# Second stage of dilated attention: bias tables through SP, values written in token order by PE, merge sums on POOL, last merge by PE

## The chip, the cores and the metric

The kernel runs on one core of a Trainium2 chip. The metric is the device time of one execution in microseconds (us). Three runs of the kernel before took 2099.55, 2100.16 and 2105.69 us; their median, 2100.16, is the number to which the changed kernel is compared.

## The reference

Two layers on 1024 tokens of 1024 channels, in float32. Layer 0 is a gated short convolution. Layer 1, to whose second half the change belongs, is a dilated attention in three groups of 16 heads of 64 channels:

```python
proj = h @ w_in                                   # h = rms_norm(x, attn_norm)
for g, (window, dilation) in enumerate(((128, 1), (512, 4), (2048, 16))):
    q = rms_norm(qkv[:, :, g, 0], q_gain[g]); k = rms_norm(qkv[:, :, g, 1], k_gain[g])
    o, l = dilated_group_attention(q, k, qkv[:, :, g, 2], bias_g, window, dilation)
    outs.append(o); lses.append(l)                # l: log of the softmax denominator
alpha = jax.nn.softmax(stack(lses), axis=0)
o = sum(alpha[..., None] * stack(outs), axis=0)
y = o * silu(z)
x = x + y @ w_out
```

In each group a query sees the keys t - dilation * j for j from 0 to 128, so that the tokens of one residue class form a dense sequence with a causal band, worked in blocks of 128 queries with a learned bias per distance. The three groups' outputs are merged with weights that come from their softmax denominators, gated by silu(z), and multiplied by w_out.

## The kernel before, in words

**First stage (to about 1645 us).** The convolution layer and the projections of the attention layer run as large matrix products. Their results are written to DRAM: q and k of each head pair and group to `qkd`, values to `vd`, the gate to `zd`, the residual stream to `x1d`. The change does not touch this stage, and the order of instructions on every engine is the same up to its end.

**Second stage.** It is written out by hand in the order of a software pipeline: inside `tc.manual_schedule` each engine runs its instructions in the order of the code. The work is 8 head pairs (two heads on partitions 0 to 63 and 64 to 127) x 3 groups = 24 units. Groups 0 and 1 have four steps per unit (two query blocks each), group 2 two (four blocks each), so that a pair has 10 steps and the whole 80. The code calls the parts of a step at different lags. In iteration k it issues

- A of step k (L886 to L897): PE multiplies q and k into a PSUM tile `ps`; DVE adds the bias table `bt` and takes the minimum in one instruction per query block (L894); ACT takes the exponential and its row sum (L897);
- C of step k - 3 (L915): PE multiplies the values `V` with the transposed probabilities `pts` into `po`; every half of a unit, `finish` copies `po` to the SBUF tile `o` (L928, L930, L933). Rows of groups 1 and 2 are in the order of the residue classes, and this copy puts them into token order, with strides in its output;
- the merge of earlier pairs at larger lags (below);
- B of step k - 2 (L904): PE transposes the probabilities, and DVE or ACT copies them to `pts` (L843, L845);
- one tile of the output product (`some`, L1035 to L1037), if there is one in this iteration;
- the loads that begin here: q, k, V and the gate (`loads`, L829 to L835) on SP's queue six steps ahead of their unit, the bias tables (`prefetch`, L858) on POOL's queue four steps ahead. Every unit has its own bias tables, two of 128 x 256 (128 x 128 in group 2).

**The merge of a pair.** The row minima and sums (`nl`) of groups 0 and 1 are stored to DRAM (`nld`, L940, L943) and read back in the order of group 2 (`ml`, L938), at `finish` of the unit's second half. `weights` (L952 to L956) and `shares` (L965 to L970) make on DVE three weights per token and head, `fo`. POOL writes them to DRAM (`fd`, L971) and reads them back six times, spread over 64 partitions (`fb`, L976). `merge` multiplies each group's output by its `fb` (group 0 on POOL, L982; groups 1 and 2 on DVE, L984), adds the three on DVE (L987, L988) and multiplies by the gate (L989), in halves of 512 tokens; `split_y` divides the result into a high and a low part for the output product (ACT L993, DVE L994). These calls stand 11 to 14 steps behind the last step of the pair; the last pair has weights and shares earlier and merges both halves in `last`.

**Output product.** The rows of w_out are split into a high part (ACT, L62) and a low part (DVE, L63). The product runs in three passes over 16 tiles of 128 x 512: pairs 0 to 3 (12 matmuls a tile, from step 55), pairs 4 and 5 (6 matmuls, from step 75), and, after the last step, pairs 6 and 7 (6 matmuls). In the first two passes a tile's partial sum is read from `x1d` (L1054, four tiles ahead, on SP), increased on DVE (L1062) and written back (L1070, on POOL's queue). They use one PSUM buffer, `pd`. In the last pass the sum goes to the output (L1134, L1135), and the load of the partial sum four tiles on follows behind the output's DMA in SP's queue.

Of the kernel before, what the change touches and what calls it, by code (L numbers as in the profile page):

```python
# [35 lines left out]
def trunk(ctx: ExitStack, tc: tile.TileContext, a, out):  # L36
# [22 lines left out]
    def split_row(raw):  # L59
        lo = wp.tile([P, 1024], F32R, name="wlo", tag="wlo", bufs=4)  # L60
        hi = wp.tile([P, 1024], F32R, name="whi", tag="whi", bufs=4)
        nc.scalar.activation(hi, raw, AF.Copy)  # L62
        nc.vector.tensor_tensor(lo, raw, hi.bitcast(F32), op=OP.subtract)  # L63
        return hi, lo
# [752 lines left out]
    with tc.tile_pool(name="sp", bufs=3, space=PSUM) as sp, tc.tile_pool(name="ptp", bufs=2, space=PSUM) as ptp, \  # L817
# [29 lines left out]
        def attention(hp, g):  # L847
# [4 lines left out]
            def prefetch():  # L852
# [3 lines left out]
                for s in range(2):  # L856
                    b0 = ap.tile([P, 256], F32, name="bt", tag="bt", bufs=6)
                    nc.gpsimd.dma_start(b0[:, :n], sk[2 * hp + s, 127:127 + P * w]  # L858
                                        .rearrange("(i m) -> i m", m=w)[:, :n])
                    bt.append(b0)  # L860
# [8 lines left out]
            def make(js, first):  # L869
# [3 lines left out]
                def A():  # L873
# [5 lines left out]
                    for n, j in enumerate(js):  # L879
                        alone = g == 2 or (j == 0 if g == 0 else j % 2 == 0)  # L880
                        x0, nk = (n if g == 2 else 2 * n), 1 if alone else 2
                        vb = [j] if alone else [j - 1, j]
                        kv = slice(vb[0] * P, (j + 1) * P)
                        for s, hs in enumerate((lo, up)):
                            out_ = ps[s][:, x0:x0 + nk].rearrange("p a b -> p (a b)")
                            nc.tensor.matmul(out_, q[hs, j * P:(j + 1) * P], k[hs, kv], start=True, stop=True)  # L886
# [21 lines left out]
                def C():  # L908
                    if js[0] % 4 == 0:
                        u["po"] = opp.tile([P, 4, P], F32, name="po", tag="po")  # L910
                    po = u["po"]
                    V = VS[hp, g]
                    for i, (x, j, vb, f, l) in enumerate(c):
                        for s, hs in enumerate((lo, up)):
                            nc.tensor.matmul(po[hs, j % 4], V[:, vb, hs], pts[s][:, i], start=f, stop=l)  # L915
                    if js[-1] % 4 == 3:
                        finish(js[-1] // 4)
# [3 lines left out]
            def finish(q):  # L921

                if q == 0:
                    O[hp, g] = ap.tile([P, S], F32, name="o", tag="o", bufs=6)
                o = O[hp, g]
                for i in range(4):
                    if g == 0 and i == 0:
                        nc.vector.tensor_copy(o[:, q * HALF:q * HALF + HALF], u["po"].rearrange("p a b -> p (a b)"))  # L928
                    elif g == 1 and i % 2 == 0:
                        nc.vector.tensor_copy(o.rearrange("p (n s c) -> p c n s", n=2, c=4)[:, 2 * q + i // 2],  # L930
                                              u["po"][:, i:i + 2])
                    elif g == 2 and i == 0:
                        nc.vector.tensor_copy(o.rearrange("p (i r) -> p r i", r=8)[:, 4 * q:4 * q + 4], u["po"])  # L933
                if q == 0:
                    return
# [5 lines left out]
                elif g == 1:  # L941
                    for n in range(2):
                        nc.gpsimd.dma_start(nld[hp, :, 1].rearrange("(n s c) e -> n s c e", n=2, c=4)[n],  # L943
                                            u["nl"].rearrange("p (c n) e -> p n c e", n=2)[:, n])
# [14 lines left out]
            def shares():  # L959
# [4 lines left out]
                fo = sm.tile([P, 3, 2, 8], F32, name="fo", tag="fo", bufs=1)  # L964
# [5 lines left out]
                nc.vector.tensor_tensor(fo.rearrange("p w s r -> p r w s"), f, mx.to_broadcast([P, 8, 3, 2]), op=OP.mult)  # L970
                nc.gpsimd.dma_start(fd[hp].rearrange("w s (i r) -> i w s r", r=8), fo)  # L971
                for w in range(G):
                    fb = fbp.tile([P, S], F32, name="fb", tag="fb")
                    u["fb", w] = fb
# [3 lines left out]
            def merge(hf, i):  # L978

                o = [O[hp, w][:, half(hf)] for w in range(G)]  # L980
                if i == 0:
                    nc.gpsimd.tensor_tensor(o[0], o[0], u["fb", 0][:, half(hf)], op=OP.mult)  # L982
                    for w in (1, 2):
                        nc.vector.tensor_tensor(o[w], o[w], u["fb", w][:, half(hf)], op=OP.mult)  # L984
                else:
                    z = SZ[hp][:, half(hf)]
                    nc.vector.tensor_tensor(o[1], o[1], o[2], op=OP.add)  # L987
                    nc.vector.tensor_tensor(o[1], o[1], o[0], op=OP.add)  # L988
                    nc.vector.tensor_tensor(z, o[1], z, op=OP.mult)  # L989

            def split_y(hf):
                hi, lo = y2[hp][:, 0, half(hf)], y2[hp][:, 1, half(hf)]
                nc.scalar.activation(hi, SZ[hp][:, half(hf)], AF.Copy)  # L993
                nc.vector.tensor_tensor(lo, SZ[hp][:, half(hf)], hi.bitcast(F32), op=OP.subtract)  # L994

            def last(hf):
                if hf == 0:
                    y2[hp] = ap.tile([P, 2, S], F32R, name="y2", tag="y2", bufs=5)
                merge(hf, 0)
                merge(hf, 1)  # L1000
                split_y(hf)

            def ready():
                y2[hp] = ap.tile([P, 2, S], F32R, name="y2", tag="y2", bufs=5)
                for hf in range(2):
                    split_y(hf)

            steps = []
            for q in range(2):
                for js in ([[4 * q, 4 * q + 1, 4 * q + 2, 4 * q + 3]] if g == 2 else  # L1010
                           [[4 * q, 4 * q + 1], [4 * q + 2, 4 * q + 3]]):
                    st = make(js, not steps)
                    steps.append(dict(zip((0, LB, LC), st)))
                    if g == 2 and q == 1:
                        lw, ld = LC + (1 if hp == HP - 1 else 2), LC + 8
# [188 lines left out]
```

## Time and profile before

| what | value |
|---|---|
| runs of the kernel before | 2099.55, 2100.16, 2105.69 us |
| the profiled execution: own time / span | 2105.98 / 2103.9 us |
| mean granted clock of TensorE | 0.97 |
| busy share of the span: PE, DVE, ACT, POOL | 94%, 71%, 43%, 44% |
| second stage: from the first reduction (L894) to the end | 1652.35 to 2103.9 us |

The profile gives for each group of instructions its busy time, the mean of one, and the idle time ahead of it with what ended that idle time. The windows give the same by stretches of time, with the clock granted to TensorE and the share of time in which the DMA engines were busy. The shares over the whole span say little here: PE's 94% come from the first stage, and the change acts in the last 450 us alone. A busy time of PE is modelled, and a matmul counts as longer when the clock is lower.

### The profile page before, as it was taken

Reading aid. Unit: us, or ns where it says so; the run is one execution under the profiler, and the core shown is the slowest. Engines: PE = TensorE matmul, PEld = TensorE weight load, DVE = VectorE, ACT = ScalarE, POOL = GpSimd, SP = SyncE. Lnnn points to the kernel's source line nnn. Section 1 sums busy time; section 2 is a strip of 40 time slices with the busy share of each in tenths; the row PEclk is TensorE's granted clock in tenths of the full one; section 3 lists DMA queues with packets and bytes.
Section 4 is the critical chain, followed back from the end, with each engine's and each line's share of the span. In section 5 each row is a group of like instructions: output and inputs, shape, how many; then the busy total and the mean of one; then the engine's idle time right before and its main releaser. Section 6 shows DMA issues by size and latency. Waiting matters only on the chain.

```text
span 2103.9 us, 29100 instructions
## 1 busy us (share of the span) xinstructions
PE 1981.9 (94%) x9998; PEld 1599.0 (76%) x9998; DVE 1499.2 (71%) x2796; ACT 906.5 (43%) x2048; POOL 915.7 (44%) x889
## 2 busy tenths in 40 slices
PE   7999899999999999999999999999999877779976
PEld 6887688888888888788888887888888655557754
DVE  6865675666757465888996889788888466667674
ACT  5433333333335353444344343443433666665540
POOL 0456666666663113344554445444445322223331
PEclk9999999999999999999999999999999998889988
DMA  5325412112216464233332233323333565577757
GB/s 183 111 82 152 113 71 75 65 66 76 71 66 210 164 221 135 95 101 120 97 125 80 101 121 104 97 101 100 120 105 118 191 170 165 155 203 228 239 148 239
DMA packets 119619, 272.59 MB, mean 130 GB/s; under 512 B 16958, under 2 KB 17726, under 8 KB 119472
## 3 DMA queue, kind: packets, MB, share of 16 engines
q1 hardware_dynamic: 90720, 180.56, 26.0%
q0 software_dynamic: 28752, 90.18, 14.8%
q8 instruction: 78, 1.28, 0.2%
q14 instruction: 69, 0.57, 0.1%
HBM read 203.01 MB, written 76.05 MB: 133 GB/s over the span
## 4 chain that ended last, share of the span: by engine, by line
PE 60%; DVE 13%; issue 5%; DMA 5%; ACT 4%; POOL 1%; SPq 0%; DVEq 0%; ACTq 0%; POOLq 0%
PE pp L306 15%; PE pp L309 15%; PE pp L308 14%; PE pp L557 3%; PE pp L558 3%; PE pp L556 3%; PE po L915 2%; DVE ws L172 2%; DMA bt<-sk 2%; ACT xs L897 2%; PE pt L904 2%; PE ps L886 1%; DVE blkc L713 1%; DVE xs L894 1%; DVE ri L74 1%
## 5 line engine op out<-in xcount | busy, mean ns | idle before, releaser
L172 DVE TENSOR_TENSOR ws<-wr,ws 128x512 fp32r<-128x512 f32 x284 | 270.1, 953 | 130.8 <-ACT ws L171 129.4
L171 ACT ACTIVATE ws<-wr 128x512 fp32r<-128x512 f32 x284 | 178.6, 630 | 390.1 <-PE pp L309 230.3
L281 POOL TENSOR_TENSOR sr<-wr 128x512 f32<-128x512 f32 x136 | 185.8, 1366 | 253.2 <-DMA wr<-in_conv_w_in 58.2
L171 ACT ACTIVATE ws<-sr 128x512 fp32r<-128x512 f32 x272 | 169.4, 629 | 292.4 <-PE pp L309 243.9
L172 DVE TENSOR_TENSOR ws<-sr,ws 128x512 fp32r<-128x512 f32 x272 | 234.2, 868 | 83.8 <-ACT ws L171 82.2
L897 ACT ACTIVATE xs<-xs,nl 128x128 f32<-128x128 f32 (+1 forms) x384 | 168.1, 439 | 128.6 <-DVE nl L894 128.0
L318 DVE TENSOR_TENSOR f<-pp,f 128x512 f32<-128x512 f32 x204 | 139.6, 684 | 83.8 <-PE pp L309 79.1
L894 DVE CUSTOM_DVE_ANT_0 xs<-ps,bt 128x128 f32<-128x128 f32 (+1 forms) x384 | 111.2, 348 | 79.8 <-DMA bt<-sk 45.9
L314 ACT ACTIVATE f<-pp 128x512 f32<-128x512 f32 x228 | 132.4, 581 | 24.8 <-POOL blkc L685 11.4
L915 PE MATMUL po<-pts,V 128*64 128x128 f32 x1120 | 98.5, 302 | 38.8 <-DVE pts L843 27.5
L915 PEld LDWEIGHTS po<-pts,V 128*64 128x64 f32 x1120 | 72.8, 149 | 72.1 <-DVE pts L843 39.4
L718 POOL DMA_DIRECT2D qkd<-blkc x96 | 68.1, 716 | 135.2 <-DVE blkc L713 127.8
L281 POOL TENSOR_TENSOR sr<-wr,sr 128x512 f32<-128x512 f32 x68 | 89.5, 1316 | 83.3 <-issue 59.3
L886 PE MATMUL ps<-qk 64*128 64x128 f32 (+1 forms) x768 | 97.6, 366 | 28.0 <-DVE nl L894 27.9
L676 ACT ACTIVATE f<-f 128x512 f32<-128x512 f32 x96 | 60.7, 633 | 137.3 <-DVE f L318 100.5
L306 PE MATMUL pp<-blke,ws 128*128 128x512 f32 x272 | 108.4, 399 | 7.2 <-ACT f L314 7.2
L306 PE MATMUL pp<-blkg,ws 128*128 128x512 f32 x272 | 107.6, 396 | 4.3 <-ACT f L314 3.2
L308 PE MATMUL pp<-blkg,ws 128*128 128x512 f32 x272 | 106.8, 393 | 3.3 <-DVE blkg L526 3.3
L306 PE MATMUL pp<-blkf,ws 128*128 128x512 f32 x272 | 108.5, 399 | 0.7 <-ACT f L314 0.7
L308 PE MATMUL pp<-blke,ws 128*128 128x512 f32 x272 | 107.7, 396 | 0.0
L306 PE MATMUL pp<-blka,ws 128*128 128x512 f32 x272 | 107.1, 394 | 0.7 <-ACT f L314 0.7
L306 PE MATMUL pp<-blkb,ws 128*128 128x512 f32 x272 | 107.5, 395 | 0.0
(298 smaller groups left out, 5532.8 us busy)
## 6 DMA issues: line engine op xcount, KB each, us to landing
wr<-in_conv_w_in SPq DMA_DIRECT2D x128, 256.0 KB, 2.8
wr<-in_wqk SPq DMA_DIRECT2D x96, 256.0 KB, 3.0
qkd<-blkc POOLq DMA_DIRECT2D x96, 256.0 KB, 3.2
qk<-qkd SPq DMA_DIRECT2D x48, 512.0 KB, 6.7
wr<-in_conv_w_out SPq DMA_DIRECT2D x64, 256.0 KB, 3.1
f<-in_x SPq DMA_DIRECT2D x48, 256.0 KB, 4.7
wr<-in_wv SPq DMA_DIRECT2D x48, 256.0 KB, 2.9
vd<-f POOLq DMA_DIRECT2D x48, 256.0 KB, 2.4
```

Of the source, the lines that this page charges most:

```text
L171: nc.scalar.activation(t[:, 0], src, AF.Copy)
L172: nc.vector.tensor_tensor(t[:, 1], src, t[:, 0].bitcast(F32), op=OP.subtract)
L281: nc.gpsimd.tensor_tensor(t, x, y, op=op)
L306: nc.tensor.matmul(ps, w[:, 0, ws], b[:, k, 0], start=new and k == 0, stop=False, skip_group_check=not new)
L308: nc.tensor.matmul(ps, w[:, 0, ws], b[:, k, 1], start=False, stop=False, skip_group_check=not new)
L309: nc.tensor.matmul(ps, w[:, 1, ws], b[:, k, 0], start=False, stop=end and k == 3, skip_group_check=not new)
L314: nc.scalar.activation(t, ps, AF.Copy)
L318: nc.vector.tensor_tensor(m, ps, m, op=OP.add)
L886: nc.tensor.matmul(out_, q[hs, j * P:(j + 1) * P], k[hs, kv], start=True, stop=True)
L894: nc.vector.tensor_tensor_reduce(out=x, in0=ps[s][:, x0:x0 + nk].rearrange("p a b -> p (a b)"), in1=u["bt"][s][:, bs], op0=OP.add, op1=OP. ...
L897: nc.scalar.activation(x, x, AF.Exp, bias=nm, scale=-1.0, accum_out=L)
L915: nc.tensor.matmul(po[hs, j % 4], V[:, vb, hs], pts[s][:, i], start=f, stop=l)
```

## The change

Six things change, all in the second stage.

1. The bias tables go through SP's queue, ahead of q, k and V of their own unit, six steps before it begins (before: POOL's queue, four steps).

In SP's queue, at the loads of three units in the middle of the stage, stood before (`qk` are q and k, two DMAs; `sz` is the gate):

```order
L829 DMA qk<-qkd 128x1024 x2
L832 DMA V<-vd 128x512 x2
L835 DMA sz<-zd 128x1024
L829 DMA qk<-qkd 128x1024 x2
L832 DMA V<-vd 128x512 x2
```

and now, for the same units (`sk_83`, `sk_84` and `sk_85` are the bias tables of groups 0, 1 and 2):

```order
L831 DMA qk<-qkd 128x1024 x2
L834 DMA V<-vd 128x512 x2
L837 DMA sz<-zd 128x1024
L860 DMA bt<-sk_83 128x256 x2
L831 DMA qk<-qkd 128x1024 x2
L834 DMA V<-vd 128x512 x2
L860 DMA bt<-sk_84 128x256 x2
```

Each unit's two bias DMAs now stand in SP's queue between the previous unit's loads and its own.

In POOL's queue, from the shares of one pair to those of the next, stood before:

```order
L971 DMA fd<-fo 128x6x8
L976 DMA fb<-fd 64x1024 x6
L940 DMA nld<-nl 128x8x4
L858 DMA bt<-sk_83 128x256 x2
L943 DMA nld<-nl 512x1x4 x2
L982 TENSOR_TENSOR o<-o,fb 128x512
L858 DMA bt<-sk_84 128x256 x2
L982 TENSOR_TENSOR o<-o,fb 128x512
L938 DMA ml<-nld 128x64
L858 DMA bt<-sk_85 128x128 x2
L971 DMA fd<-fo 128x6x8
L976 DMA fb<-fd 64x1024 x6
```

and now:

```order
L979 DMA fd<-fo 128x6x8
L983 DMA fb<-fd 64x1024 x6
L945 DMA nld<-nl 128x8x4
L948 DMA nld<-nl 512x1x4 x2
L1010 TENSOR_TENSOR o<-o 128x1024 x2
L943 DMA ml<-nld 128x64
L979 DMA fd<-fo 128x6x8
L983 DMA fb<-fd 64x1024 x6
```

The three pairs of bias DMAs have left the queue, and the two products of 512 columns have become two sums of 1024.

2. The products of values write token order. Group 1 goes through its blocks in another order (`b`), and the matmul of groups 1 and 2 writes `po` with a stride; group 2 has two matmuls of 64 columns, one for each half of the tokens, where it had one of 128. `finish` is one contiguous copy of 128 x 512 (six per pair).

3. Minima and sums are stored one step after the last scores of a unit (`store`, lag 1), weights follow at lag 3 and shares at lag 4 (before 5 and 6). The spread shares of group 2 are read back first.

4. The merge has whole rows of 1024: three products on DVE (`both`, lags 8, 9 and 10), two sums on POOL (`add`, lags 9 and 10), the gate on DVE (lag 11), the high part on ACT (lag 12), the low part on DVE (lag 13). `o` has five buffers, not six. The output product's first pass begins at step 54 and its second at step 74, one step earlier than before. Weight rows are split at other steps, with the low part one step after the high part.

5. The last pair's shares are not spread through DRAM. `wide` copies them to rows of 64 equal values (ACT twice, DVE once), 48 transposes on PE turn these into PSUM tiles (`scale`), and DVE multiplies with these. `last` follows one and two steps after the shares.

6. In the last two passes tiles alternate between the banks `ps` and `pd` once the last scores are done (`k` odd, from step 81). The partial sums of the last pass are loaded from the second pass on into the buffers of `qk` and `V` that are no longer used; in the last pass nothing is loaded, and the output goes out from these.

On DVE, from the last pair's shares to the last pass, stood before (`o<-o,fb` is a product, `o<-o` a sum):

```order
L970 TENSOR_TENSOR fo<-f,mx 128x8x6
L1062 TENSOR_TENSOR part<-pd,part 128x512 x6
L984 TENSOR_TENSOR o<-o,fb 128x512 x2
L987 TENSOR_TENSOR o<-o 128x512
L988 TENSOR_TENSOR o<-o 128x512
L989 TENSOR_TENSOR sz<-o,sz 128x512
L994 TENSOR_TENSOR y_17731<-sz,y_17731 128x512
L1062 TENSOR_TENSOR part<-pd,part 128x512
```

and now:

```order
L975 TENSOR_TENSOR fo<-f,mx 128x8x6
L994 COPY fb<-fo 128x1024
L1107 TENSOR_TENSOR part<-ps,part 128x512
L1007 TENSOR_TENSOR o<-o,pd 128x512
L1007 TENSOR_TENSOR o<-o,ps 128x512 x2
L1030 TENSOR_TENSOR o<-o 128x512 x2
L1031 TENSOR_TENSOR sz<-o,sz 128x512
L1033 TENSOR_TENSOR y_17742<-sz,y_17742 128x512
L1107 TENSOR_TENSOR part<-pd,part 128x512
```

Between the shares and the first merged half stood six tiles of the second pass; now stands one, and the products read their shares from PSUM.

The diff, cut to its core:

```diff
-                    nc.gpsimd.dma_start(b0[:, :n], sk[2 * hp + s, 127:127 + P * w]
+                    nc.sync.dma_start(b0[:, :n], sk[2 * hp + s, 127:127 + P * w]
...
+                        b = 2 * (j % 4) + j // 4 if g == 1 else j
...
+                            if g == 2:
+                                for q in range(2):
+                                    nc.tensor.matmul(u["po", q][hs].rearrange("p (i r) -> p r i", r=8)[:, j],
+                                                     V[:, vb, hs], pts[s][:, i, q * 64:q * 64 + 64], start=f, stop=l)
+                                continue
+                            po = u["po", j // 4][hs]
+                            po = po.rearrange("p (s c) -> p c s", c=4) if g == 1 else \
+                                po.rearrange("p (b t) -> p b t", b=4)
+                            nc.tensor.matmul(po[:, j % 4], V[:, vb, hs], pts[s][:, i], start=f, stop=l)
...
+                nc.vector.tensor_copy(O[hp, g][:, half(q)], u["po", q])
...
+            def both(w):
+                nc.vector.tensor_tensor(O[hp, w], O[hp, w], u["fb", w], op=OP.mult)
...
+            def scale(w, hf, pool, name):
...
+                for r in range(8):
+                    nc.tensor.transpose(fb.rearrange("p (i r) -> p r i", r=8)[:, r],
+                                        u["wide", w][hs, r].rearrange("p s d -> p (s d)"), ident[hs, hs])
+                o = O[hp, w][:, half(hf)]
+                nc.vector.tensor_tensor(o, o, fb, op=OP.mult)
+
+            def add(i, eng=nc.gpsimd):
+                eng.tensor_tensor(O[hp, 1], O[hp, 1], O[hp, i], op=OP.add)
...
+            end.setdefault(1, []).append(store)
+            if g == 2:
+                todo = [(LC, weights), (LC + 1, shares)]
+                if hp == HP - 1:
+                    todo += [(LC + 1, wide), (LC + 2, lambda: last(0)), (LC + 3, lambda: last(1))]
+                else:
+                    todo += [(LC + 1, spread_shares), (LC + 5, lambda: both(2)), (LC + 6, lambda: both(1)),
+                             (LC + 6, lambda: add(2)), (LC + 7, lambda: both(0)), (LC + 7, lambda: add(0)),
+                             (LC + 8, gate), (LC + 9, high), (LC + 10, low)]
...
-        LD = LC + 12
+        LD = LC + 11
...
+            if n >= 19:
+                piece(n + 13)
+            if k >= len(steps) + 1 and k % 2:
+                ps = sp.tile([P, 4, P], F32, name="ps", tag="ps").rearrange("p a b -> p (a b)")
+            else:
+                ps = pp1.tile([P, HALF], F32, name="pd", tag="pd")
...
-            begins.setdefault(max(-1, k - 6), []).append(lambda un=un: loads(*un))
-            begins.setdefault(max(-1, k - 4), []).append(prefetch)
+            begins.setdefault(max(-1, k - 6), []).extend([prefetch, lambda un=un: loads(*un)])
...
-                        piece(j + 4)
```

More of the change, by code (lines that the diff above doesn't have):

```diff
@@ L908, in C @@
                 def C():
-                    if js[0] % 4 == 0:
-                        u["po"] = opp.tile([P, 4, P], F32, name="po", tag="po")
-                    po = u["po"]
+                    for q in ((0, 1) if g == 2 else (js[0] // 4,)):
+                        if js[0] == 0 or (g < 2 and js[0] == 4):
+                            u["po", q] = opp.tile([P, HALF], F32, name="po", tag="po")
                     V = VS[hp, g]
@@ L923, in finish, with store @@
                 if q == 0:
[L924 to L935, printed above, removed]
+                    O[hp, g] = ap.tile([P, S], F32, name="o", tag="o", bufs=5)
+                nc.vector.tensor_copy(O[hp, g][:, half(q)], u["po", q])
+            def store():
                 if g == 2:
@@ L991, in split_y, with wide @@
[L991 to L994, printed above, removed]
+            def both(w):
+                nc.vector.tensor_tensor(O[hp, w], O[hp, w], u["fb", w], op=OP.mult)
+            def wide():
+                for w in (2, 1, 0):
+                    t = u["wide", w] = fbp.tile([P, 8, 2, 64], F32, name="fb", tag="fb")
+                    src = u["fo"][:, w].rearrange("p s r -> p r s")[:, :, :, None].to_broadcast([P, 8, 2, 64])
+                    if w == 1:
+                        nc.vector.tensor_copy(t, src)
+                    else:
+                        nc.scalar.activation(t, src, AF.Copy)
@@ new lines, in add, with gate, high, low @@
+            def add(i, eng=nc.gpsimd):
+                eng.tensor_tensor(O[hp, 1], O[hp, 1], O[hp, i], op=OP.add)
+            def gate():
+                nc.vector.tensor_tensor(SZ[hp], O[hp, 1], SZ[hp], op=OP.mult)
+            def high():
+                y2[hp] = ap.tile([P, 2, S], F32R, name="y2", tag="y2", bufs=5)
+                nc.scalar.activation(y2[hp][:, 0], SZ[hp], AF.Copy)
+            def low():
+                nc.vector.tensor_tensor(y2[hp][:, 1], SZ[hp], y2[hp][:, 0].bitcast(F32), op=OP.subtract)
@@ L998, in last @@
                     y2[hp] = ap.tile([P, 2, S], F32R, name="y2", tag="y2", bufs=5)
[L999 to L1006, printed above, removed]
+                h, z = half(hf), SZ[hp][:, half(hf)]
+                for w, bank in ((2, (pp1, "pd")), (1, (sp, "ps")), (0, (sp, "ps"))):
+                    scale(w, hf, *bank)
+                for w in (2, 0):
+                    nc.vector.tensor_tensor(O[hp, 1][:, h], O[hp, 1][:, h], O[hp, w][:, h], op=OP.add)
+                nc.vector.tensor_tensor(z, O[hp, 1][:, h], z, op=OP.mult)
+                nc.scalar.activation(y2[hp][:, 0, h], z, AF.Copy)
+                nc.vector.tensor_tensor(y2[hp][:, 1, h], z, y2[hp][:, 0, h].bitcast(F32), op=OP.subtract)
             steps = []
@@ L1109, in trunk @@
         k = 0
-        while k < len(steps) + LC + 9 or any(x >= k for x in extra):
-            for lag in (0, LC, *range(LC + 1, LC + 12), LB):
-                if 0 <= k - lag < len(steps) and lag in steps[k - lag]:
-                    steps[k - lag][lag]()
+        while k < len(steps) + LC + 3 or any(x >= k for x in extra):
+            for lag in (0, 1, LC, *range(LC + 1, LC + 11), LB):
+                for f in steps[k - lag].get(lag, ()) if 0 <= k - lag < len(steps) else ():
+                    f()
             if k in extra:
@@ L1118, in trunk @@
             k += 1
+        for j in range(45, 48):
+            piece(j)
         banks = [(sp, "ps")] * 3 + [(ptp, "pt")] * 2 + [(opp, "po")] * 2 + [(pp1, "pd")]
```

106 lines of the change are left out of this document (48 added, 58 removed).

## The prediction

> **What bounds the kernel now.** The profiled execution took 2105.98 us, 2.1 more than its span, and lies 5.8 above the median of the three runs, 2100.16. So I sum against the span and subtract the saving from the median. About 0.3% is what a measurement of this kernel can tell from no change.
>
> ```profile
> span 2103.9 us, 29100 instructions
> ```
>
> Everything up to 1645 us is untouched, so I cut the rest into windows: one for each of the head pairs 0 to 4, from first bias-and-minimum reduction (L894) to the next pair's; steps 50 to 54; steps 55 to 70 (16 dense tiles); steps 71 to 79; the end. Columns: stretch, length, busy PE, PE load, DVE, ACT, POOL, granted clock, DMA share, GB/s.
>
> ```profile
> 1652.30:1680.95 28.65, 27.01 (x244) 19.38 (x244) 18.34 (x104) 25.89 (x105) 4.74 (x8) 0.93 0.51 162
> 1680.95:1723.55 42.60, 33.56 (x328) 24.79 (x328) 23.37 (x119) 29.59 (x117) 12.66 (x19) 0.97 0.70 201
> 1723.55:1770.55 47.00, 36.08 (x306) 26.70 (x306) 30.52 (x131) 29.90 (x114) 12.66 (x19) 0.83 0.55 149
> 1770.55:1817.15 46.60, 36.36 (x306) 27.07 (x306) 30.52 (x131) 29.90 (x114) 12.68 (x19) 0.83 0.59 163
> 1817.15:1865.75 48.60, 35.25 (x306) 26.33 (x306) 30.52 (x131) 29.90 (x114) 12.65 (x19) 0.85 0.63 169
> 1865.75:1894.70 28.95, 21.52 (x153) 16.04 (x154) 24.34 (x68) 18.41 (x54) 1.64 (x3) 0.72 0.62 204
> 1894.70:1981.40 86.70, 86.63 (x662) 66.91 (x662) 56.76 (x228) 47.26 (x187) 29.96 (x48) 1.00 0.80 242
> 1981.40:2025.00 43.60, 35.57 (x300) 26.47 (x298) 33.36 (x126) 29.18 (x105) 14.65 (x23) 0.92 0.58 177
> 2025.00:2103.90 78.90, 52.68 (x222) 38.46 (x222) 41.46 (x67) 6.21 (x13) 14.47 (x23) 0.83 0.62 199
> ```
>
> Pairs 2 to 4 take 46.6 to 48.6 us, while DVE and ACT have 30 us of work each: waits bind. Only steps 55 to 70 are bound by an engine, PE (86.63 of 86.70, so 5.42 a step). The waits of 1640 to 1865 (total, times, longest) and the chain behind one of them (start, length, what) name the culprit:
>
> ```profile
> POOL fd L971 <- DVE fo L970: 85.1, 4, 23.0
> DVE xs L894 <- DMA bt<-sk: 35.2, 5, 11.4
> ```
>
> ```profile
> 1701.17 3.34 DMA fd<-fo
> ...
> 1706.12 9.78 DMA fb<-fd
> ...
> 1718.36 1.29 POOL o L982
> 1720.08 6.88 DMA bt<-sk
> ```
>
> The bias tables are issued by POOL, in order, behind fd and fb, which wait for DVE's shares, and behind a merge product that waits for fb. They then start late, and DVE, with ACT and PE behind it, stands still once per pair. What a pair costs without that is seen in pair 1 up to its wait:
>
> ```profile
> 1681.00:1713.60 32.60, 30.42 (x306) 22.82 (x306) 23.36 (x119) 28.04 (x111) 7.58 (x13) 1.00 0.59 183
> ```
>
> Ten steps in 32.6 us, full clock, PE nearly full at 30.42.
>
> **The change part by part.**
>
> *Bias tables by SP, two steps earlier.* They now stand ahead of qk and V of their own unit, six steps (about 20 us) before use. Landing, from 1700 to 1841:
>
> ```profile
> qk<-qkd SPq DMA_DIRECT2D x18, 512.0 KB, 8.4
> ...
> bt<-sk POOLq DMA_DIRECT2D x12, 128.0 KB, 10.6
> ...
> nld<-nl POOLq DMA_DIRECT2D x6, 8.0 KB, 10.2
> ml<-nld POOLq DMA_DIRECT2D x3, 32.0 KB, 3.4
> ```
>
> Even 10.6 us is covered by 20, so the wait of 7 to 11 us per pair goes. Queued behind the two issues are qk and V; the second qk tile of a pair's first unit gets its buffer only three steps (10 us) before use, against 8.4: the next thing to be late. The Trainium skill, page "DMA: Bandwidth & Descriptors", section "Issuing engines are not separate DMA queues", says that another issuing engine saves only the time of issuing. Read strictly that speaks against this part; I weigh it as a rival. At the start the table no longer comes after POOL's last tail work:
>
> ```profile
> 1648.45 1.28 ACT L897 ACT_TABLE_LOAD   x1
> 1649.30 3.20 POOL L858 DMA_DIRECT2D bt<-sk  x6
> ...
> 1652.69 0.40 ACT L897 ACTIVATE xs<-xs,nl 128x128 f32<-128x128 f32 x1 [2.95 <-DVE nl L894]
> ```
>
> The first exponential then waits only for ACT's own table, until 1649.73: 2.9 us saved.
>
> *DVE work per pair.* Groups of 1700 to 1841 (three pairs), then two groups of 1860 to 2025 for 1024 columns:
>
> ```profile
> L984 DVE TENSOR_TENSOR o<-o,fb 128x512 f32<-128x512 f32 x12 | 7.7, 682 | 0.0
> L933 DVE COPY o<-po 128x512 f32<-128x512 f32 x6 | 6.5, 1091 | 2.1 <-PE po L915 2.1
> L930 DVE COPY o<-po 128x256 f32<-128x256 f32 x12 | 6.5, 618 | 0.0
> ...
> L988 DVE TENSOR_TENSOR o<-o 128x512 f32<-128x512 f32 x6 | 4.2, 693 | 0.6
> ...
> L928 DVE COPY o<-po 128x512 f32<-128x512 f32 x6 | 4.1, 690 | 0.6 <-PE po L915 0.6
> ```
>
> ```profile
> L63 DVE TENSOR_TENSOR wlo<-wraw,whi 128x1024 fp32r<-128x1024 f32 x7 | 8.6, 1225 | 5.7 <-ACT whi L62 5.7
> ```
>
> ```profile
> L62 ACT ACTIVATE whi<-wraw 128x1024 fp32r<-128x1024 f32 x7 | 7.3, 1046 | 0.0
> ```
>
> Finishing copies: 6 x 0.69 = 4.1 in place of 2 x 0.69 + 4 x 0.62 + 2 x 1.09 = 6.0, so -1.9. Sums to POOL: -4 x 0.69 = -2.8. Products: 3 x 1.23 in place of 4 x 0.68, +1.0. Gate and low part whole: -0.3. Together -4.0, DVE 26.5. ACT stays at 29.9, so PE and ACT now set the pair.
>
> *POOL.* Its products of 512 columns give the price of the sums:
>
> ```profile
> L982 POOL TENSOR_TENSOR o<-o,fb 128x512 f32<-128x512 f32 x6 | 8.0, 1327 | 0.0
> ```
>
> Two sums of 1024: 4 x 1.33 = 5.3 in place of 2.7, with the bias issues gone; POOL keeps over half its time free. The gate stands a step behind the last product; 1.23 + 2.65 against 3.5 makes it wait 0.4. POOL's sum can also meet a DVE product, as products met before:
>
> ```profile
> 1922.17 2.15 DVE L984 TENSOR_TENSOR o<-o,fb 128x512 f32<-128x512 f32 x2
> ```
>
> ```profile
> 1921.84 1.33 POOL L982 TENSOR_TENSOR o<-o,fb 128x512 f32<-128x512 f32 x1
> ```
>
> Two products took 2.15 in place of 1.36: 0.8 lost. The new sum over columns is twice as long, so 0 to 2.65 a pair; DVE's slack hides most, I take 0.5. The Trainium skill, page "SBUF — State Buffer", section "Who interferes with whom", says that a DVE instruction with two SBUF inputs contends with a GpSimd one that reads SBUF, one input not. These rows agree; by it alone the full 2.65 would fall on each overlapping product, 7 pairs x 2.65 = 19 us.
>
> *Token order by PE.* Group 2's 16 products per pair become 32 of 64 columns, groups 1 and 2 write PSUM with strides. One batch, and eight transposes, at full clock:
>
> ```profile
> 1749.23 1.02 PE pt L904 x8
> ...
> 1751.11 1.09 PE po L915 x16
> ```
>
> That is 68 ns a record; a product makes two. Half-width ones cost between half and full: 0 to 32 x 0.068 = 2.2 us a pair; I take 1.1. No row shows a strided PSUM write. The nearest is DVE's strided copy, 1.09 against 0.69 or 1.58 times; of the 112 records now strided (7.6 us) that would be +4.4 a pair. Contiguous writes would be 0. I take 0, since no row has PE slowed by where it writes, and keep 4.4 for the range.
>
> *Weights and stores earlier.* The maxima (nld) are stored one step after their scores, in POOL's queue behind at most a sum (2.65). From there nld 10.2 + ml 3.4 = 13.6 stands against four steps of 3.5 = 14 until the weights on DVE; fd 3.34, its issue, two fb issues and a landing of 5 to 9.8 make 10 to 15 against 14 for the first product. Both just fit: nothing in the sum, up to 3 us a pair as a rival. Behind both stand the next reductions on DVE.
>
> *So a pair with merges:* PE 30.42 + 1.1 = 31.5; pair 1's 2.2 of gaps; 0.9 for port and gate, and 0.4 for rounding up: 35 (32 to 38).
>
> *Sum, before to after.* Start -2.9. Pair 0 unchanged. Pair 1 42.6 to 32.7: -9.9. Pairs 2 to 4 to 35 each: -12.0, -11.6, -13.6. Steps 50 to 54: four of 4.5 (pair steps with a weight split, 1.05 ACT and 1.23 DVE) and one dense of 5.4, 23.4: -5.5. Steps 55 to 70: dense starts a step sooner, so 15 x 5.42 + 3.9 = 85.2: -1.5. Steps 71 to 79: three of 3.9, six of 4.3 (PE 3.0 plus six dense matmuls at 0.217), 37.5: -6.1.
>
> *The end.* Chain, last values product, and a window of the last matmuls (7.80 us for 36, 0.217 each):
>
> ```profile
> 2035.47 1.09 PE L915 MATMUL po<-pts,V 128*64 128x128 f32 x16
> ```
>
> ```profile
> 2052.74 6.55 DMA x1d<-part
> ...
> 2091.36 5.25 DMA out_x<-part
> ```
>
> ```profile
> 2074.00:2081.80 7.80, 7.80 (x36) 1.00 0.39 132
> ```
>
> Now, the last values are done at 2036.6 and 67 us follow: spreading shares through memory, partial sums that go out and come back, and buffers that wait for output. After: with X the start of step 79, values end at X + 14. Copies, weights and shares 4, wide copies 2, 48 transposes at 0.13 = 6, partly under dense tiles, two chains of 3 products, 2 sums, gate and split (5.5 each): with part additions about 24 until the last dense tile. Then 96 x 0.217 = 21 and 6 for the last sum and output: X + 65, that is 60.7 after step 79 (X + 4.3): -18.2. If the transposes hide entirely, X + 59; if the single pd bank holds PE for both chains, X + 73.
>
> Together 2.9 + 9.9 + 37.2 + 5.5 + 1.5 + 6.1 + 18.2 = 81.3: a span of 2022.6, a median of 2100.2 - 81.3 = **2019 us**.
>
> **The rivals.**
> - *New waits take over (0.13).* Pairs 2 to 4 move 7.0 to 8.2 MB (47.0 x 149 to 48.6 x 169), at 35 us 200 to 234 GB/s. Steps 55 to 70 ran at 242 unharmed, but at 5.4 us a step. If qk, ml or fb is 5 to 9 late a pair: +15 to 27 on pairs 2 to 4, +3 to 5 in steps 71 to 79: 2037 to 2051.
> - *POOL blocks DVE (0.07).* One product a pair held for the whole 2.65, and the gate for 1, less the 0.9 taken, on seven pairs: 19, so 2038. For it: the 0.8 above. Against: the 8 us of slack that DVE has in a pair of 35.
> - *The wait stays (0.05).* If the queue saves only issue time, 6 x 0.55 = 3.3 a pair, then pairs 1 to 4 give back 47.1 - 13.2 = 34: 2053. Against it, the lead of six steps.
> - *Strided writes cost as DVE's do (0.05).* 4.4 x 8 = 35 at most, a part under ACT: 2044.
> - *Slower than before: strided writes by several times.* 112 records, 7.6 us a pair. At 2.3 times, 10 us a pair, the 81 us are gone (0.02 for no change within 0.3%). At 3 times, 15.2 x 8 = 122: 2141 (0.08). No row excludes it; that PE never slowed in this trace except by clock speaks against.
>
> **How the numbers follow.** The forecast has 0.60; its own range is 2000 (pairs 32, end X + 59, steps 71 to 79 3 shorter) to 2036 (pairs 38, end X + 73). Faster: 0.60 + 0.13 + 0.07 + 0.05 + 0.05 = 0.90; same 0.02; slower 0.08. The range 2000 to 2053 takes in all but the strided cases and a low tail.
>
> **What would show it.** Right: no wait of L894's line for bt, pairs 2 to 4 at 32 to 38 us with clock near 1.0, dense steps of 5.4, last values about 50 us before the end. Wrong: DVE waiting for qk, ml or fb; DVE products over 1.3 us beside POOL; values batches of groups 1 and 2 above 1.1 us for 16 records; the dense stretch above 5.6 a step; PE idle over 10 us in the last 50.

## The result, and the profile after

The changed kernel took 2044.94 us (median of four runs, 2041.18 to 2046.98) against 2099.86: a ratio of 0.973, 95% interval 0.9708 to 0.9753, or 55 us less. Forecast was 2019, 81 us less.

The profiled execution of the changed kernel, 2041.18, is its fastest, that of before, 2105.98, its slowest. Part of their difference lies in the untouched first stage: the first matmul of the second stage starts at 1645.6 us before and at 1642.6 now. So I compare second stages, from that matmul to the end: 458.3 us before, 396.5 in this profile, and 407.0 in another profile of the same kernel, taken on another chip in an execution of 2059.29 (the run "changed kernel again" below).

The windows of the changed kernel: pairs 0 to 4, steps 50 to 53, the 16 steps with 12 dense matmuls (54 to 69), steps 70 to 73, 74 to 78, and from step 79 to the end. Columns as in the prediction. The first row begins at 1646.00, 2.4 us after pair 0's first reduction (1643.55).

```profile
1646.00:1675.70 29.70, 25.72 (x232) 19.00 (x232) 15.73 (x91) 26.55 (x108) 2.82 (x5) 0.94 0.68 223
1675.70:1712.40 36.70, 33.25 (x354) 25.72 (x354) 25.30 (x121) 29.53 (x114) 11.38 (x13) 0.95 0.70 197
1712.40:1748.80 36.40, 29.57 (x330) 22.66 (x328) 27.49 (x123) 29.41 (x113) 11.03 (x14) 1.00 0.78 207
1748.80:1784.00 35.20, 30.16 (x338) 23.10 (x334) 27.38 (x122) 28.64 (x112) 10.48 (x14) 1.00 0.73 209
1784.00:1825.60 41.60, 31.62 (x338) 23.92 (x338) 32.87 (x124) 30.55 (x113) 13.89 (x15) 0.97 0.75 215
1825.60:1844.50 18.90, 14.40 (x154) 11.32 (x154) 14.63 (x53) 14.28 (x47) 0.00 (x0) 0.87 0.66 225
1844.50:1934.30 89.80, 89.25 (x718) 69.93 (x720) 53.35 (x212) 48.20 (x188) 30.43 (x40) 1.00 0.81 245
1934.30:1950.30 16.00, 12.23 (x154) 9.42 (x150) 14.32 (x51) 12.84 (x41) 1.32 (x3) 1.00 0.65 227
1950.30:1974.80 24.50, 23.66 (x210) 18.39 (x211) 17.75 (x63) 16.24 (x60) 10.78 (x15) 1.00 0.79 220
1974.80:2039.10 64.30, 51.73 (x304) 41.42 (x302) 40.14 (x77) 10.40 (x27) 9.31 (x14) 0.89 0.60 213
```

Pairs 2 and 3 came from 47 to 36 us with the clock back at 1.00. Pair 4 did not: 41.6. DVE's waits from 1640 to 1845 no longer have a row for the bias tables:

```profile
DVE xs L897 <- PE ps L889: 24.1, 27, 2.5
...
DVE xs L897 <- ACT y L1017: 6.3, 3, 2.1
DVE xs L897 <- ACT pts L847: 5.9, 2, 5.4
...
DVE xs L897 <- DMA nld<-nl: 2.4, 1, 2.4
```

The last row is new: a first reduction that waits until a store of minima and sums has landed, since `nl` has three buffers and the one it needs is still being read by that store. This small row leads to the main finding.

### The profile page after: what moved, and what is told of

Its sections match the earlier page's. It is cut to its first block, busy times and chain, and to the rows that moved or that the text cites. A ratio compares the mean times of both kernels' runs of the same rounds, so it can differ in the third digit from the quotient of the medians.

```text
span 2039.1 us, 29660 instructions
## 1 busy us (share of the span) xinstructions
PE 1957.8 (96%) x10302; PEld 1591.1 (78%) x10302; DVE 1480.3 (73%) x2734; ACT 906.6 (44%) x2043; POOL 898.4 (44%) x832
## 3 DMA queue, kind: packets, MB, share of 16 engines
q8 instruction: 81, 1.33, 0.3%
## 4 chain that ended last, share of the span: by engine, by line
PE 64%; DVE 11%; issue 5%; ACT 4%; DMA 3%; POOL 0%; DVEq 0%; ACTq 0%; POOLq 0%; SPq 0%
PE pp L308 15%; PE pp L311 15%; PE pp L310 15%; PE pp L559 3%; PE pp L560 3%; PE pp L558 3%; DVE ws L174 2%; PE pt L907 2%; ACT xs L900 2%; PE po L926 2%; PE ps L889 2%; DVE blkc L715 1%; PE pd L1063 1%; PE pd L1064 1%; PE pd L1065 1%
## 5 line engine op out<-in xcount | busy, mean ns | idle before, releaser
L316 ACT ACTIVATE f<-pp 128x512 f32<-128x512 f32 x228 | 132.5, 581 | 27.4 <-POOL blkc L687 13.3
L308 PE MATMUL pp<-blke,ws 128*128 128x512 f32 x272 | 107.7, 396 | 6.8 <-ACT f L316 6.8
L308 PE MATMUL pp<-blkg,ws 128*128 128x512 f32 x272 | 107.6, 396 | 4.8 <-ACT f L316 3.9
L310 PE MATMUL pp<-blkg,ws 128*128 128x512 f32 x272 | 106.8, 392 | 3.3 <-DVE blkg L528 3.3
L310 PE MATMUL pp<-blke,ws 128*128 128x512 f32 x272 | 107.3, 394 | 0.0
L311 PE MATMUL pp<-blke,ws 128*128 128x512 f32 x272 | 107.1, 394 | 0.0
L308 PE MATMUL pp<-blkd,ws 128*128 128x512 f32 x272 | 107.0, 393 | 0.0
L311 PE MATMUL pp<-blkg,ws 128*128 128x512 f32 x272 | 106.4, 391 | 0.0
```

The source lines that it names most:

```text
L308: nc.tensor.matmul(ps, w[:, 0, ws], b[:, k, 0], start=new and k == 0, stop=False, skip_group_check=not new)
L310: nc.tensor.matmul(ps, w[:, 0, ws], b[:, k, 1], start=False, stop=False, skip_group_check=not new)
L311: nc.tensor.matmul(ps, w[:, 1, ws], b[:, k, 0], start=False, stop=end and k == 3, skip_group_check=not new)
L316: nc.scalar.activation(t, ps, AF.Copy)
```

## The experiments

Twelve runs in three groups, each group on one chip with the kernel before beside it. Ratios are to that; "stage" is the second stage in the profile. The kernel before took 2108.45, 2109.39 and 2109.49 us in the three groups (medians), 9 us more than beside the changed kernel above, so runs of different groups are compared by their ratios, not by their times.

**Bias tables, undone and alone.** Undone in the changed kernel:

```diff
-                    nc.sync.dma_start(b0[:, :n], ...
+                    nc.gpsimd.dma_start(b0[:, :n], ...
-            begins.setdefault(max(-1, k - 6), []).extend([prefetch, lambda un=un: loads(*un)])
+            begins.setdefault(max(-1, k - 6), []).append(lambda un=un: loads(*un))
+            begins.setdefault(max(-1, k - 4), []).append(prefetch)
```

> The changed kernel with one part undone: the bias tables go through POOL's queue again, four steps ahead. Theory (the wait of DVE for the bias tables was what held the pairs, and their place behind fd and fb on POOL made it): the wait comes back at 6 to 11 us a pair in pairs 1 to 4, pairs of 43 to 47 us, 2080 to 2090 us. Rival (the shorter DVE work and the earlier weights made the gain, the queue is nearly free, as POOL's merge products that waited for fb are gone): within 10 us of the changed kernel, 2045 to 2055.

Measured: 2070.70 us, 0.9817 (0.9796 to 0.9838), stage 422.3. That is 0.9 points, about 18 us, above the changed kernel, between theory and rival; in the profile pairs 1 to 4 take 41.4 to 45.1 us, nearer to the theory. The wait is back, but at 4.3 to 6.3 us a pair in place of 8.2 to 11.4, and at another unit: group 2's.

```profile
1720.77 0.29 DVE L897 CUSTOM_DVE_ANT_0 xs<-ps,bt 128x128 f32<-128x128 f32 x1 [6.18 <-DMA bt<-sk]
```

The reverse edit, alone in the kernel before:

> The kernel before with one part done alone: the bias tables through SP, six steps ahead, in front of q, k and V. Theory (the queue and the lead are the cause): the wait for bt goes, pairs 1 to 4 come to 37 to 40 us and the start is 3 us earlier, together 35 to 40 us less, 2060 to 2065. Rival (another issuing engine saves only the time of issuing, 3.3 us a pair): 2083 to 2090. Second rival (fb is then the late one, DVE's merge products wait for it in the place of bt): a wait of 5 us or more a pair at the products, about 2080.

Measured: 2103.66 us, 0.9982 (0.9968 to 0.9997), stage 454.3. Only 4 us were gained, 2.3 of them up to pair 1's first reduction and 1.7 in pair 1. Theory and both rivals miss: pairs 2 to 4 take 142.1 us together, against 142.2 before. The pause is still there, 9.6 us ahead of the pair's first reduction, for something else. The reduction, then the POOL queue:

```profile
1717.59 0.29 DVE L894 CUSTOM_DVE_ANT_0 xs<-ps,bt 128x128 f32<-128x128 f32 x1 [9.64 <-DMA nld<-nl]
```

```profile
1699.87 3.13 POOL L976 DMA_DIRECT2D fb<-fd  x6 [2.17 <-DMA fd<-fo]
1702.99 0.93 POOL L940 DMA_DIRECT2D nld<-nl  x1
```

The store of pair 1's group 0, 16 KB, is issued behind fd and six fb transfers and lands 14.4 us later, at 1717.36; the reduction starts 0.23 us after that. In the next two pairs the store lands at 1763.16 and 1811.05, and the reductions start at 1763.40 and 1811.28. There the profile names a transfer of q and k as what ended the wait; but these transfers belong to a later unit and land after the reductions, at 1764.51 and 1812.39, and PE had written the scores 4 to 5 us before. So it is the store here too.

In the kernel before, the same store landed at 1722.40, 1769.74 and 1816.67, and the bias table 0.4 to 1.1 us after it. Two waits lay on one spot, and the profile shows only the one that ends last.

**The two waits, one and both.** In the kernel before, without and with the bias edit:

```diff
-                u["nl"] = sm.tile([P, 8, 4], F32, name="nl", tag="nl", bufs=3)
+                u["nl"] = sm.tile([P, 8, 4], F32, name="nl", tag="nl", bufs=4)
```

> The kernel before with four buffers for the minima and sums (nl) in place of three, and nothing else; the bias tables stay on POOL. Theory (two waits lie on the same spot: the first reduction of a pair needs its bias table and an nl buffer that is free once its store has landed, and both transfers stand behind fd and fb on POOL): nothing gained, pairs 2 to 4 at 46 to 49 us, within 5 us of the kernel before. Rival (the nl buffer alone was the wait, the bias table only came beside it): pairs of 37 to 40, 30 us faster.

> The kernel before with both: the bias tables through SP six steps ahead, and four nl buffers. Theory (each wait hid behind the other, so that only both together give the gain): the pauses of 11 to 13 us ahead of pairs 2 to 5 go, pairs 1 to 4 at 35 to 39 us, the second stage 35 to 45 us shorter than in the kernel before. Rival (fb or ml is the next one late at the same place): a wait of 5 us or more a pair remains at the merge products or at the weights, 10 to 20 us shorter.

Measured: buffers alone 2107.70 us, 0.9995 (0.9983 to 1.0008), stage 457.1: nothing. Both: 2079.22 us, 0.986 (0.9845 to 0.9875), stage 428.7: 30 us. The theory holds in kind: only both together help. Its size does not: 35 to 45 us were expected, and pairs 2 to 4 take 39.5 to 44.0 where 35 to 39 were. The rival's waits for `fb` are there too, but short, 8.5 us in four. Pair 1, then pairs 2 to 4 together, of both, and pairs 2 to 4 of the buffers alone:

```profile
1679.55:1712.45 32.90, 30.68 (x306) 22.81 (x306) 23.38 (x119) 28.35 (x113) 8.74 (x13) 1.00 0.63 183
1712.45:1836.55 124.10, 100.47 (x918) 75.07 (x918) 91.74 (x393) 89.07 (x344) 29.07 (x40) 0.90 0.74 187
```

```profile
1727.15:1866.45 139.30, 106.84 (x918) 79.31 (x918) 91.52 (x393) 89.72 (x342) 38.09 (x57) 0.84 0.62 162
```

Gains of 0.2%, 0.05% and 1.4%: the parts do not add. Pairs at 41 and a clock of 0.90 leave something to the rest of the change; which part of it takes pairs 2 and 3 down to 36 is open.

**Token order, undone.** PE writes `po` without strides, DVE's copies for groups 1 and 2 have them, as before:

```diff
-                            nc.tensor.matmul(po[:, j % 4], V[:, vb, hs], pts[s][:, i], start=f, stop=l)
+                            nc.tensor.matmul(po[hs, j % 4], V[:, vb, hs], pts[s][:, i], start=f, stop=l)
...
+                        nc.vector.tensor_copy(o.rearrange("p (i r) -> p r i", r=8)[:, 4 * q:4 * q + 4], po)
```

> The changed kernel with one part undone: PE writes the values in the order of the residue classes and DVE brings groups 1 and 2 into token order in its copies, as before. Theory (DVE is one link of the ring DVE, ACT, PE that sets a pair of 35 us, and PE's strided writes cost nothing): DVE's copies 1.9 us longer a pair, half of it seen outside the dense steps, 2047 to 2055. Rival (strided PSUM writes cost PE as much as strided copies cost DVE, 4 us a pair): faster, 2020 to 2035.

Measured: 2051.18 us, 0.9733 (0.9717 to 0.9749), stage 400.5: the same as the changed kernel. Token order was worth nothing that shows; neither was it dear. In the changed kernel a batch of group 1 with stride takes what a contiguous one took (1.09), and 32 half-width records of group 2, with another stride, little more (group 2's row first):

```profile
1715.95 1.20 PE L920 MATMUL po<-pts,V 128*64 128x64 f32 x32 [1.30 <-DVE pts L845]
```

```profile
1780.39 1.10 PE L926 MATMUL po<-pts,V 128*64 128x128 f32 x16 [0.91 <-DVE pts L845]
```

**Sums on DVE.** One default value is changed:

```diff
-            def add(i, eng=nc.gpsimd):
+            def add(i, eng=nc.vector):
```

> The changed kernel with one part undone: the two sums of the merge run on DVE in place of POOL. Theory (POOL's sums take work off the ring, but hold up the low parts of weight rows 0, 1, 6 and 7, 1.2 to 1.8 us each, as both read two SBUF operands): the low parts take 1.22 again, and 2.4 us a pair more on DVE in the five pairs without dense tiles: 2045 to 2053. Rival (DVE has slack, sums on POOL buy nothing): 2037 to 2041, 6 us faster.

Measured: 2054.68 us, 0.9752 (0.9734 to 0.9769), stage 402.0. Some 0.2 points above the changed kernel, with intervals that overlap: POOL's sums help by a few us at most, and the rival, 6 us faster, is out. As expected, all eight low parts of the weight rows take 1.21 to 1.23 us here, where four of them are stretched beside POOL's sums (below).

**The end, part by part.** Shares of the last pair through DRAM:

```diff
-                    todo += [(LC + 1, wide), (LC + 2, lambda: last(0)), (LC + 3, lambda: last(1))]
+                    todo += [(LC + 1, spread_shares), (LC + 8, lambda: last(0)), (LC + 9, lambda: last(1))]
...
-                    scale(w, hf, *bank)
+                    nc.vector.tensor_tensor(O[hp, w][:, h], O[hp, w][:, h], u["fb", w][:, h], op=OP.mult)
```

> The changed kernel with one part undone: the last pair's shares go through DRAM (fd, fb) as before and are merged at the later steps, while the partial sums of the last pass are still loaded early. Theory (the way through DRAM was on the path, about 12 us of transfer against 5 us of copies and transposes, partly under dense tiles): from step 79 to the end 70 to 75 us in place of 64, 6 to 11 us slower than the changed kernel. Rival (the dense tiles cover it): within 3 us.

Measured: 2053.97 us, 0.9737 (0.972 to 0.9753), stage 401.5, and 65.5 us from step 79 to the end against 64.3 and 65.2 in the two profiles of the changed kernel. The rival is right: the dense tiles cover the way through DRAM.

Partial sums loaded late:

```diff
-            if n < 28:
-                piece(n + 4)
-            if n >= 19:
-                piece(n + 13)
+            piece(n + 4)
...
                         nc.sync.dma_start(out[dt, :, half(hf)], part[j])
+                        piece(j + 4)
```

> The changed kernel with one part undone: the partial sums of the last pass are loaded four tiles ahead behind the output's transfers, as before, while the last pair is still merged through PE. Theory (the last pass was held by transfers that stand behind one another in SP's queue): from step 79 to the end 70 to 74 us in place of 64, 6 to 10 us slower. Rival (the loads only ran beside the matmuls): within 3 us.

Measured: 2057.93 us, 0.9751 (0.9733 to 0.9769), stage 412.2, of which the end:

```profile
1988.05:2061.10 73.05, 52.08 (x304) 41.54 (x302) 40.33 (x77) 10.29 (x27) 9.31 (x14) 0.82 0.57 191
```

The same work as in the changed kernel's last window, 52 us of PE, takes 73.05 in place of 64.3; the eight other profiles with early loads lie at 63.0 to 65.5. So 8 to 9 us of the 17.8 by which the end became shorter go with the early loads in the profiles. The medians show less, 0.2 points or 4 to 5 us, with intervals that overlap; the profiled execution is this run's slowest. The way through DRAM, undone, cost about 1. The rest, some 8 us, I have not taken apart; alternating banks and the earlier last merge are candidates that were not tried alone. Each part was undone alone, and as with the two waits above, such parts need not add.

**What held the pairs that stayed long.** The changed kernel's chain around step 48, and its SP queue ahead of it (start, time from first to last issue):

```profile
1810.87 11.05 DMA wraw<-in_wo
...
1821.94 1.06 ACT whi L62
```

```profile
1799.11 10.74 SPq L831 DMA_DIRECT2D qk<-qkd  x2
1809.94 0.88 SPq L834 DMA_DIRECT2D V<-vd  x2
1810.87 15.17 SPq L56 DMA_DIRECT2D wraw<-in_wo  x3
```

The weight row stands behind a q and k transfer that waits for its buffer, is issued at 1810.87, lands at 1821.9, and ACT waits 4.75 us. Then DVE's low parts meet POOL's sums:

```profile
1816.28 3.00 DVE L66 TENSOR_TENSOR wlo<-wraw,whi 128x1024 fp32r<-128x1024 f32 x1
```

```profile
1815.85 2.35 POOL L1010 TENSOR_TENSOR o<-o 128x1024 f32<-128x1024 f32 x1 [2.70 <-DVE o L986]
```

The subtraction ends at 1819.28, 1.08 us after the sum. So it is with all seven DVE instructions on two SBUF operands that began while a POOL sum ran in this profile, four low parts and three merge products: each ends 1.08 to 1.09 us after the sum, as if its work began only then. DVE's additions to the partial sums, with one operand in PSUM, kept their 0.68 to 0.69 beside the same sums.

The changed kernel again, and three kernels that build on it: rows fetched one a step from step 39 and from step 64, into four buffers, with five buffers for partial sums to make room, so that these are loaded three tiles ahead in place of four; then the low parts of rows 0, 1, 6 and 7 two steps later; then four nl buffers.

```diff
+        for kt in range(8):
+            when((k1 - 15 if kt < 4 else k2 - 10) + kt % 4, fetch, (kt,))
...
-            when(k - 4, fetch, (kt,))
...
-            when(k + 1, split_low, kt)
+            when(k + {0: 3, 1: 3, 6: 3, 7: 3}.get(kt, 1), split_low, kt)
```

> The changed kernel once more, on the same chip as the three runs beside it: 0.973 of the kernel before. All theories expect the second stage at 396 to 405 us in the profile; it is what the next three are compared with.

> The changed kernel with the eight weight rows of the output product fetched one a step from step 39 and 64 on, into four buffers in place of two (and five buffers of partial sums in place of six, to make room); where they are split stays. Theory (the row fetched for step 48 stands on SP behind q and k that wait for a buffer, lands late, and ACT with everything behind it waits 4.8 us): step 48 to 49 at 4 to 5 us in place of 7, pair 4 at 36 to 38 in place of 41 to 42, 4 to 6 us faster than the changed kernel. Rival (the transfers are what is short, not the order; earlier rows only push q, k and V back): pair 4 the same or other pairs longer, within 2 us.

> As the run with early rows, and the low parts of rows 0, 1, 6 and 7 on DVE two steps later, when POOL's two sums are over. Theory (DVE's subtraction and POOL's sum each read two SBUF operands and shut each other out): the low parts at 1.22 each in place of 2.4 to 3.06, 6.2 us of DVE time less, 3 to 5 us faster than early rows alone. Rival (DVE stretched because it was waiting for something else, or had slack there): the same durations, or the same time, within 1 us.

> As the run before it, and four nl buffers in place of three. Theory (a store of minima that lands late still holds the first reduction of pair 2, 2.4 to 3.5 us in the profiles): pair 1 at 34 to 35 in place of 37 to 38, 2 to 3 us faster again, in all 0.967 to 0.969 of the kernel before. Rival (the next wait, for fb or ml, comes at the same place): no change, within 1 us.

| run | us | ratio (interval) | stage | pairs 1, 2, 3, 4 |
|---|---|---|---|---|
| changed kernel again | 2051.63 | 0.9728 (0.9711 to 0.9744) | 407.0 | 38.0, 37.1, 41.7, 42.4 |
| rows early | 2047.45 | 0.9707 (0.9693 to 0.972) | 398.4 | 38.1, 36.7, 37.5, 39.4 |
| low parts later | 2046.24 | 0.9696 (0.9682 to 0.9709) | 393.3 | 36.7, 39.0, 37.7, 38.1 |
| four nl buffers | 2040.61 | 0.967 (0.9657 to 0.9683) | 391.0 | 35.0, 37.0, 35.7, 37.3 |

Each step down is small, with an interval that overlaps its neighbour's or nearly meets it; from first to last they are apart, 11 us. The changed kernel's stage, 407.0, is 2 above what was expected of it. With early rows ACT's wait for them is gone. The time fell by 4.2 us, within the 4 to 6 expected; pair 4, at 39.4, lost 2 to 3 of them and did not reach the 36 to 38 expected. The low parts, duration as smallest, median and largest, in the changed kernel and with the low parts later:

```profile
L66 DVE TENSOR_TENSOR wlo<-wraw,whi x8: 1211/1817/3056, 1816.3 to 1978.3; 128x1024 fp32r<-128x1024 f32 x8
```

```profile
L66 DVE TENSOR_TENSOR wlo<-wraw,whi x8: 1215/1216/1221, 1836.3 to 1993.6; 128x1024 fp32r<-128x1024 f32 x8
```

The stretching is gone entirely, as the theory has it; in time 1.2 us came of it, against 3 to 5 expected. The run with early rows still had 4.8 us of stretching, so most of it lay beside other work. The fourth buffer brought 5.6, more than expected. The repeated run of the changed kernel shows that the wait comes and goes: there pair 2 begins without it, but pair 4 has it, and a chain piece names it.

```profile
1785.46 14.32 DMA nld<-nl
```

From 1785.46 it ends at 1799.78, and pair 4's first reduction starts at 1800.00, 1.9 us after PE had its scores ready. Pair 3 took 41.7 us there, so this is a part of it only; DVE's products also waited for fb, 7.7 us in all from 1640 to 1848. In pairs 1 to 4 of the two profiles the store of group 0 landed 7.0 to 14.3 us after its issue; whether that is in time is a matter of a few us, which fits the changed kernel's scatter between executions; that it is the whole of it isn't shown.

The last kernel beats both others. It also lost 4 us in a dense step, where a load of a partial sum landed late: it was issued at 1922.44, behind a weight row, and landed at 1931.96.

```profile
1932.09 0.69 DVE L1107 TENSOR_TENSOR part<-pd,part 128x512 f32<-128x512 f32 x1 [4.11 <-DMA part<-x1d]
```

Its 16 dense steps take 95.2 us, the changed kernel's 89.8. Whether the shorter lead with five buffers or the weight row ahead of the load made it late was not tried.

## Why the prediction was right or wrong, by its own steps

*The sign, the stated range (2000 to 2053) and the end hold; the size was 26 us too large.* The measured 2045 lies above the forecast's own range (2000 to 2036) and inside that of the first rival, new waits (2037 to 2051, chance 0.13). So the stated range held because the rivals were taken into it, which is partly luck. The rival's mechanism did not come as described either: it had qk, ml or fb 5 to 9 us late a pair, while DVE's products waited for fb 0.97 us in all in one profile and 7.7 in the other. New waits came, but for the `nl` store and for a weight row.

*Start: right.* The first exponential stands 4.1 us behind the first matmul, 7.1 before, and the bias edit alone gives these 3 us, of which 2.3 are left at pair 1's first reduction.

*Bias tables by SP: this step failed.* "So the wait of 7 to 11 us per pair goes" did not follow from the lead of six steps: alone, the edit left the pause standing, on another transfer. The prediction named q and k as next to be late; it was the buffer of `nl`. The trace of before held the hint: the same POOL queue that delayed bt carried the nld stores, which landed 10.2 us after issue in the median, and the one that counts landed at most 1.1 us ahead of bt in pairs 2 to 4. What I did not ask is which buffers those stores release.

*Weights and stores earlier: priced at nothing, and by the traces a large part of the gain hangs on it.* With the bias edit and the fourth buffer in the kernel before, the store of group 0 in pairs 2 and 3 is issued 33 to 34 us after the pair's first reduction and lands at 47.5 and 49.7, when the next pair has long begun (39.5 and 40.5); by these times three buffers would have held that pair 8 to 9 us. In the changed kernel fd, fb and the stores come two steps earlier: the store is issued at 24.6 and 24.5 and lands at 35.1 and 33.5, 1.3 and 1.8 us before the next pair, and only one pair still waits 2.4 us. That the fourth buffer removes the wait in the kernel before is shown by the runs; that the earlier weights and stores do it in the changed one is argued from these times. They were not tried by themselves, and neither was the removal of POOL's products that waited for fb.

*The rival that the queue saves only issue time: refuted, by its price.* It forecast 3.3 us a pair. The bias edit alone got none in pairs 2 to 4, and with four nl buffers the same edit is worth 28 us, 5.9 a pair over pairs 1 to 4. What the other queue saves is waiting behind instructions that wait, and that is more than the time to issue. The Trainium skill, page "DMA: Bandwidth & Descriptors", section "Issuing engines are not separate DMA queues", says that starting DMAs on several engines saves only the time of issuing them. The bias edit alone looks like this rule; the two edits together do not agree with it.

*Pair 1 at 32.7: wrong by 4 to 5.* The first merge product moves from lag 11 to lag 8, so pair 0's products and sums now fall in pair 1's last three steps. I moved the instructions and left the pair's price. In one profile 2.4 us of it are the nl wait; with four nl buffers on top of the other row edits pair 1 takes 35.0, and 32.9 in the kernel before with both edits, where the merge stays out of it.

*Pairs 2 to 4 at 35: right for 2 and 3 in one execution (36.4, 35.2), 6.6 short for pair 4, and 6.7 and 7.4 for pairs 3 and 4 in the other.* Two of the four weight rows now fall into pair 4, at steps 47 to 49, the second of them late from SP's queue; I had put all four into steps 50 to 53. Pair 3's 41.7 is explained in part only, by the nl wait of 2.9.

*DVE 26.5, PE 31.5, ACT 29.9:* DVE came to 27.4, PE to 30, ACT to 29. Sums of 1024 on POOL took 2.35, not 2.65.

*DVE against POOL: right in kind, wrong in place.* The products were hardly touched: 18 of 21 stayed at 1.21 to 1.22, three took 1.29 to 1.33. The low parts of four weight rows were stretched to 2.41 to 3.06. This is what the section "Who interferes with whom" of the Trainium skill's page "SBUF — State Buffer" says of two SBUF inputs. The expectation that this costs much on the path failed: taking away 4.8 us of stretching gave 1.2 us of time, with intervals that overlap.

*Token order: 1.1 us a pair on PE for half-width, 1.9 off DVE's copies.* 32 half-width records take 1.20, so 64 take 2.4 where 32 whole ones took 2.2: 0.2 a pair. Strided writes cost 0, as taken; both rivals that rested on them are refuted. What DVE saved bought nothing that the times show: undone, token order gave the same time.

*Dense steps at 5.42: 5.61.* That is just past the 5.6 that I had named as a sign of being wrong. The price came from a stretch that began with a step of 3.7 us. Pair 6, dense throughout, takes 55.7 us before (from 1920.1) and now (from 1878.6); there was no gain to be had.

*Steps 70 to 78:* 40.5 in place of 37.1; low parts of rows 6 and 7 met POOL's sums here too.

*The end at X + 65: measured X + 64.3, in part by other reasons.* The last values stand 50.0 us before the end, as forecast. But I credited the way through DRAM, and that was covered: undone, it cost about 1 us. Early loads gave up to half, by the profiles.

*Scatter.* The second stage is 61.8 us shorter in one profile of the changed kernel and 51.3 in the other; the medians' 55 lie between. I built the sum on single executions, so about 7 of the 26 us are the choice of execution, and some 19 the steps above: 4 in pair 1, 8 in pairs 2 to 4, and 7 from step 50 to 78.

## What to carry to other kernels

When an engine waits at one spot, list everything that the waiting instruction needs there, with the transfers that release its output buffers, and look when each would have been ready. Two waits on one spot hide each other: here removing either gave 0.2% and 0.05%, removing both 1.4%, so a part that "did nothing" alone may still be needed. Costs fall where the schedule now puts them: after moving a lag, price the stage into which its work has moved.

## What the runs showed of the hardware

- The same 16 KB store of minima and sums (bias edit alone) landed 5.0 us after its issue in pair 0, with no `fb` ahead of it; 13.6 to 16.0 us in pairs 1 to 4, issued right behind six transfers of 256 KB on the same queue; and 7.2 to 8.2 us in pairs 5 to 7, behind the same six. So these alone do not set it; what else does was not tried.
- PE's writes to PSUM with a stride of 4 elements cost nothing: 16 records in 1.10 us against 1.09 contiguous. With a stride of 8 and half the width, 32 records took 1.20.
- A DVE instruction on two SBUF operands that began while a POOL sum ran ended 1.08 to 1.09 us after that sum (seven of seven in the changed kernel's profile): a subtraction of 1.22 us became 2.41 to 3.06, and the POOL sum kept its 2.35. Where DVE began first (early rows, at 1831.06, POOL 0.22 us later), DVE kept its 1.21 and the POOL sum took 3.20.
- One POOL sum of 1024 columns, 2.35 us, is shorter than two products of 512, 2.65.
